# Padding the heads of two activation pools so that activations and split weights share an offset modulo 512 bytes

## The chip, the cores and the metric

The kernel runs on one core of a Trainium2 chip. The metric is the device time of one execution in microseconds. Before the change it is 2132.72 us, the median of 3 runs (2131.33 to 2134.95).

## The reference

One layer of a streaming encoder trunk on x of 256 rows by 2048 features, all in float32, then a last norm.

```python
for l in range(DEPTH):                                   # DEPTH = 1
    h = rms_norm(x, norm_mix_g[l])
    x = x + hybrid_mixer(h, positions, w_in[l], conv_w[l], ..., w_out[l])
    h = rms_norm(x, norm_x_g[l])
    mem_n = rms_norm(mem, norm_mem_g[l])
    x = x + cross_attention(h, mem_n, w_xq[l], w_xkv[l], w_xo[l])
    h = rms_norm(x, norm_ffn_g[l])
    x = x + jnp.square(jax.nn.relu(h @ w_ff1[l])) @ w_ff2[l]
return rms_norm(x, norm_final_g)
```

The mixer projects h once (2048 by 18464 weights) and runs two token mixers side by side, a chunked retention with 8 heads and a gated delta rule with 16 heads; both are gated, merged and projected. The cross-attention has 4 heads over 256 memory rows. The MLP has 8192 hidden features. Nearly all of the work is products of 256 rows with weights of 2048 by some thousand columns.

## The kernel before, in words

Every large product is made in three parts. A float32 operand is split into a high part, rounded by ScalarE to the type that TensorE takes at full rate (L89 for weights, L96 and others for activations), and a low part, the rest, made by VectorE (L90, L97). The product is high by high, high by low and low by high.

Weights come by DMA into `raw` (three buffers of 8192 bytes a partition) and are split in two halves into `whi` and `wlo` (three buffers of 4096 bytes each); the function is `fetch`. Activations lie in quads: `new_quad` makes one tile of 128 partitions by 4 by 512 words, 8192 bytes a partition, which holds four blocks of 128 features; in each block 256 columns of the high part stand beside 256 of the low part.

Two functions multiply.

- `chunk` gives 512 columns of output with rows on the partitions. The activations are the stationary operand (128 columns, 512 bytes), the weights the moving one (512 columns). Each product is three matmuls, L130, L131 and L132. One call is 96 matmuls. It is used for the memory's values, the retention's values, the gates, and the second MLP matrix.
- `blocks` gives 128-column blocks of output with features on the partitions. The weights are the stationary operand (one block of 128 columns, 512 bytes of `whi` or `wlo`), the activations the moving one. A pair of matmuls makes a product: L168 streams 512 columns (high and low part at once) against `whi`, L169 streams 256 columns against `wlo`. One call for two blocks is 32 pairs. It is used for the memory's keys, the mixer's other projections, `w_out`, `w_xq`, `w_xo` and the first MLP matrix.

A matmul of one line is followed at once by that of the next, so the time from a line's first start to its last, divided by the steps between, is the time of one pair or of one triple.

Quads lie in three pools. `hq` (five quads) holds h1, the normed x of the mixer, for the mixer's whole time; then the merged output, the attention's output and the MLP's hidden features. `kv` holds `memq`, four quads of the normed memory, at the start. `q2` holds four quads: h2 (the input of `w_xq`), then h3 (the input of the first MLP matrix). In the very last call of `chunk`, which is called with `hold=quad_b`, the split weights of two of the four fetches go into quads of `q2` too (L84 to L86).

Pools lie one behind the other in each partition, each behind those that are open when it is opened: `const`, `wpipe` (raw, whi, wlo), `hq`, `small`; then `mixc` and `kv` (closed after the memory's keys), in whose place `mix` comes, behind `mixc`; when `mix` and `mixc` are closed, `tail` (the residual, 16384 bytes) comes behind `small`, then `q2`. A pool's size is the sum of its tags, each its largest tile times its buffers.

The order of the instructions on every engine is found before the kernel runs, by a planner that works through the program by priority with estimated durations; a tile with a tag waits for a free buffer of that tag. `blocks` ends with an evacuation of each block in front of other work (`high_priority`): ScalarE writes `bo` (tag `bo`, two buffers), VectorE adds the other half of PSUM, and the caller's function reads `bo`.

In the delta rule's `gdn_stream`, which is called for four groups of two pairs of heads, four small instructions for each pair (L563) take the diagonal of a gram matrix: they write a product that nobody reads into `dj`, and keep its row sums in `ssk`. `dj` is a tile of 512 bytes with a buffer of its own in the pool `mix`.

Of the kernel before, what the change touches and what calls it, by code (L numbers as in the profile page):

```python
# [10 lines left out]
F32 = mybir.dt.float32  # L11
# [6 lines left out]
P = 128  # L18
D = 2048
S = 256  # L20
# [8 lines left out]
C_GQ, C_GK, C_GV = 6144, 8192, 10240  # L29
C_GA, C_GZ, C_TA, C_TB = 12288, 12320, 14368, 16416  # L30
THETA = 10000.0
TWO_PI = 2.0 * math.pi
BIG = 1.0e30


def _short(v, bits):
    m, e = math.frexp(v)
    return math.ldexp(math.floor(m * (1 << bits)), e - bits)


PI_1 = _short(TWO_PI, 12)
PI_2 = _short(TWO_PI - PI_1, 11)
PI_3 = float(np.float32(TWO_PI - PI_1 - PI_2))
MAGIC = 1.5 * 2.0**23
# [3 lines left out]
def trunk(ctx: ExitStack, tc: tile.TileContext, x, mem, positions, norm_mix_g, w_in, conv_w, gdn_a_log, gdn_dt_bias,  # L48
# [4 lines left out]
    act, vec, pool, pe = nc.scalar, nc.vector, nc.gpsimd, nc.tensor  # L53

    cp = ctx.enter_context(tc.tile_pool(name="const", bufs=1))
    wp = ctx.enter_context(tc.tile_pool(name="wpipe", bufs=3))
    hqp = ctx.enter_context(tc.tile_pool(name="hq", bufs=1))
    sm = ctx.enter_context(tc.tile_pool(name="small", bufs=2))
# [8 lines left out]
    def bank():  # L67
        return psp.tile([P, 512], F32, name="b", tag="b", bufs=4)
# [38 lines left out]
    def new_quad(pl, bufs):  # L107
        both = pl.tile([P, 4, 2 * S], F32R, name="q", tag="q", bufs=bufs)
        quad = Quad((both[:, :, 0:S], both[:, :, S:2 * S]))
        quad.both = both  # L110
        return quad
# [137 lines left out]
    kv = kvs.enter_context(tc.tile_pool(name="kv", bufs=2))  # L249
# [18 lines left out]

    kt_d = dram.tile([P, KT, S], F32, name="kt_d", tag="kt_d", bufs=1)
    vv_d = dram.tile([P, NT, D], F32, name="vv_d", tag="vv_d", bufs=1)  # L270
    memq = [new_quad(kv, 4) for _ in range(4)]
    ssqm = cp.tile([P, NT, 4], F32, name="ssqm")

# [87 lines left out]
    def rounded(o, i, scale):  # L361
        vec.tensor_scalar(o, i, scale, MAGIC, op0=ALU.mult, op1=ALU.add)
        vec.tensor_scalar(o, o, -MAGIC, None, op0=ALU.add)

    def less(k, c):
        vec.scalar_tensor_tensor(av, k, -c, av, op0=ALU.mult, op1=ALU.add)

    rounded(hv, av, 1.0 / (4096.0 * TWO_PI))
    less(hv, 4096.0 * PI_1)
    vec.scalar_tensor_tensor(lv, hv, -4096.0 * PI_2, av, op0=ALU.mult, op1=ALU.add)  # L370
    rounded(lv, lv, 1.0 / TWO_PI)
    less(lv, PI_1)
# [131 lines left out]
    mx = mixer.enter_context(tc.tile_pool(name="mix", bufs=2))  # L504
# [14 lines left out]
    def gdn_stream(grp):  # L519
# [5 lines left out]
        for pr in range(2):  # L525
# [16 lines left out]
            for b in range(2):  # L542
                kh = mx.tile([P, 2, S], F32R, name="kh", tag="kh", bufs=2)
                kl = mx.tile([P, 2, S], F32R, name="kl", tag="kl", bufs=2)
                sq = mx.tile([P, S], F32, name="sq", tag="acc", bufs=2)
                act.activation(kh, kq[:, b], AF.Copy)
                vec.tensor_sub(kl, kq[:, b], kh.bitcast(F32))
                act.activation(sq, kq[:, b, 1], AF.Square)
                g0, g1 = bank(), bank()
                g0v = g0.rearrange("p (a n) -> p a n", a=2)  # L550
                g1v = g1[:, 0:256].rearrange("p (a n) -> p a n", a=2)
                if b == 0:
                    ssq = g1[:, 256:260].rearrange("p (b i) -> p b i", b=2)
                for t in range(NT):
                    pe.matmul(ssq[:, b, t:t + 1], sq[:, t * P:(t + 1) * P], ones[:, :1], start=True, stop=True)
                for n, (l, r) in enumerate(((kh, kh), (kh, kl), (kl, kh))):
                    pe.matmul(g0v, l[:, 0, 0:P], r, start=n == 0, stop=n == 2)  # L557
                for n, (l, r) in enumerate(((kh, kh), (kh, kl), (kl, kh))):
                    pe.matmul(g1v, l[:, 0, P:S], r[:, :, P:S], start=n == 0, stop=n == 2)
                grams.append((g0v, g1v))  # L560
                for t, src in enumerate((g0v[:, 0, 0:P], g1v[:, 0, :])):
                    dj = mx.tile([P, P], F32, name="dj", tag="dj", bufs=1)
                    vec.scalar_tensor_tensor(dj, src, 1.0, ident, op0=ALU.mult, op1=ALU.mult,  # L563
                                             accum_out=ssk[:, b, t:t + 1])
            ske = mx.tile([P, 2, NT], F32, name="ske", tag="ske", bufs=2)
# [214 lines left out]
    for j in range(5):  # L780
        if j < 4:
            group = gdn_stream(j)
        if prev is not None:
            if j < 4:
                quad = mx.tile([P, 4, S], F32, name="mg", tag="mg", bufs=3)
                kept.append(quad)
            else:
                quad = quad_a()
            gates(j - 1, prev[0], prev[1], quad, take_back if j == 4 else None)
        if j < 4:  # L790
            yr = mx.tile([P, NT, 512], F32, name="yr", tag="yr", bufs=1)
            yg = mx.tile([P, NT, 512], F32, name="yg", tag="yg", bufs=1)
            retention(j, yr)
            gdn_core(j, *group, yg)
            prev = (yr, yg)
# [5 lines left out]
    tp = ctx.enter_context(tc.tile_pool(name="tail", bufs=2))  # L801
    rt = tp.tile([P, KT, S], F32, name="rt", tag="rt", bufs=1)
    q2p = ctx.enter_context(tc.tile_pool(name="q2", bufs=1))

    def quad_b():
        return new_quad(q2p, 4)
# [181 lines left out]
def _inv_freq():  # L988
    e = np.arange(0, RDK, 2, dtype=np.float32) / np.float32(RDK)
    return (np.float32(1.0) / np.power(np.float32(THETA), e)).astype(np.float32)  # L990

# [17 lines left out]
```

## Time and profile before

| what | value |
| --- | --- |
| median of 3 runs | 2132.72 us (2131.33 to 2134.95) |
| the profiled execution, whole | 2133.46 us |
| its span, first instruction to last | 2131.7 us |
| instructions | 28768 |
| granted TensorE clock, mean | 0.999 |

The profiled execution lies 0.74 us above the median, and 1.8 us of it lie outside the span. Times in rows are microseconds from the start of the span. The busy time of TensorE (PE) counts a matmul until its modelled end, so matmuls overlap in it: the distance of starts, not the duration, is what one costs.

### The profile page before, as it was taken

What the parts mean: (1) busy time and instruction counts of PE and PEld (TensorE: products, weight loads), DVE (VectorE), ACT (ScalarE), POOL (GpSimd) and SP (SyncE); (2) the same over time, 40 slices, a digit from 0 to 9 for tenths busy, and PEclk for the clock granted to TensorE, in tenths of its full rate; (3) what the DMA queues carried; (4) which work ended last, traced back from release to release, by engine and by line L of the source; (5) the groups of instructions that cost most, each with busy time, mean ns of one, the idle gap of its engine ahead of it and who ended that gap; (6) DMA issues with size and microseconds to landing.
All of it is one profiled execution on the core that took longest, in us unless ns stands there. A gap on an engine that the chain in (4) does not pass through costs nothing.

```text
span 2131.7 us, 28768 instructions
## 1 busy us (share of the span) xinstructions
PE 2102.5 (99%) x11172; PEld 1798.5 (84%) x11172; DVE 1411.9 (66%) x2225; ACT 1092.3 (51%) x1700; POOL 30.6 (1%) x39
## 2 busy tenths in 40 slices
PE   8999999899999999999999999999999999999998
PEld 6878888788888888888888888888888888888887
DVE  6756779588678866786567666666556545655655
ACT  7565565364555445645456555554434434434444
POOL 0000000000000000000000000000000000000000
PEclk9999999999999999999999999999999999999999
DMA  8777665455545654565457654566556556556653
GB/s 296 248 235 250 198 194 184 131 172 190 177 148 198 198 187 135 180 203 181 157 178 251 204 180 157 176 188 189 193 189 191 184 193 194 180 197 191 185 197 139
DMA packets 316009, 405.91 MB, mean 190 GB/s; under 512 B 16592, under 2 KB 224480, under 8 KB 315744
## 3 DMA queue, kind: packets, MB, share of 16 engines
q1 hardware_dynamic: 315872, 404.08, 58.6%
q8 instruction: 87, 1.43, 0.3%
q14 instruction: 50, 0.41, 0.1%
HBM read 390.40 MB, written 13.65 MB: 190 GB/s over the span
## 4 chain that ended last, share of the span: by engine, by line
PE 94%; DMA 2%; ACT 1%; DVE 1%; issue 0%; POOL 0%; SPq 0%; ACTq 0%; POOLq 0%; DVEq 0%
PE s L168 32%; PE s L169 16%; PE s L131 13%; PE s L130 13%; PE s L132 13%; PE b L646 2%; DMA dec_d<-dec_w 1%; ACT dec_w L471 1%; PE b L557 1%; PE b L100 0%; ACT whi L89 0%; DVE wlo L90 0%; PE b L102 0%; PE b L101 0%; PE b L215 0%
## 5 line engine op out<-in xcount | busy, mean ns | idle before, releaser
L90 DVE TENSOR_TENSOR wlo<-raw,whi 128x1024 fp32r<-128x1024 f32 x702 | 858.1, 1223 | 523.5 <-ACT whi L89 518.3
L89 ACT ACTIVATE whi<-raw 128x1024 fp32r<-128x1024 f32 x702 | 742.8, 1059 | 724.2 <-PE s L132 370.2
L168 PE MATMUL s<-q,whi 128*128 128x512 f32 x3088 | 1080.1, 397 | 0.3 <-DVE q L898 0.3
L169 PE MATMUL s<-q,wlo 128*128 128x256 f32 x3088 | 845.4, 281 | 6.4 <-DVE wlo L90 6.4
L168 PEld LDWEIGHTS s<-q,whi 128*128 128x128 f32 x3088 | 571.4, 188 | 125.2 <-DVE q L898 0.5
L169 PEld LDWEIGHTS s<-q,wlo 128*128 128x128 f32 x3088 | 580.1, 188 | 21.9 <-DVE wlo L90 10.2
L131 PE MATMUL s<-wlo,q 128*128 128x512 f32 x1264 | 495.3, 392 | 0.2 <-DVE wlo L90 0.2
L132 PE MATMUL s<-whi,q 128*128 128x512 f32 x1264 | 492.0, 390 | 0.0
L130 PE MATMUL s<-whi,q 128*128 128x512 f32 x1264 | 450.1, 391 | 0.0
L131 PEld LDWEIGHTS s<-wlo,q 128*128 128x128 f32 x1264 | 237.9, 188 | 49.8 <-DVE wlo L90 1.2
L130 PEld LDWEIGHTS s<-whi,q 128*128 128x128 f32 x1264 | 237.6, 188 | 50.1 <-ACT q L228 0.4
L132 PEld LDWEIGHTS s<-whi,q 128*128 128x128 f32 x1264 | 237.6, 188 | 48.8
L173 ACT ACTIVATE bo<-s 128x256 f32<-128x256 f32 x193 | 73.1, 379 | 121.6 <-PE s L169 121.6
L174 DVE TENSOR_TENSOR bo<-bo,s 128x256 f32<-128x256 f32 x193 | 80.4, 417 | 54.0 <-ACT bo L173 53.7
L512 DVE SCALAR_TENSOR_TENSOR acc<-bo,cw,acc 128x255 f32<-128x255 f32 (+2 forms) x144 | 67.1, 477 | 4.7 <-ACT acc L509 3.3
L612 DVE TENSOR_TENSOR pr<-lw,tw 32x31 f32<-32x31 f32 (+15 forms) x124 | 40.5, 326 | 9.1 <-DMA lw<-scr_l 6.9
L614 DVE TENSOR_TENSOR tw<-tw,pr 32x31 f32<-32x31 f32 (+15 forms) x124 | 40.7, 328 | 2.4
L747 ACT ACTIVATE gth<-s 128x512 f32<-128x512 f32 x32 | 18.9, 592 | 23.1 <-PE s L132 17.5
L937 DVE SCALAR_TENSOR_TENSOR res<-s,rstd3q,res 128x512 f32<-128x512 f32 (+1 forms) x32 | 22.3, 735 | 12.0 <-PE s L132 12.0
L509 ACT ACTIVATE acc<-bo,cw 128x256 f32<-128x256 f32 x48 | 24.2, 504 | 7.3 <-DVE bo L174 5.1
L926 DVE SCALAR_TENSOR_TENSOR hs<-bo 128x256 f32<-128x256 f32 x64 | 27.0, 422 | 1.1
L929 DVE TENSOR_TENSOR q<-hs,q 128x256 fp32r<-128x256 f32 x64 | 26.8, 418 | 0.9 <-ACT q L928 0.9
(292 smaller groups left out, 1086.7 us busy)
## 6 DMA issues: line engine op xcount, KB each, us to landing
raw<-w_in SPq DMA_DIRECT2D x144, 1024.0 KB
raw<-w_ff SPq DMA_DIRECT2D x128, 1024.0 KB
raw<-w_xkv SPq DMA_DIRECT2D x31, 1024.0 KB
raw<-w_out SPq DMA_DIRECT2D x16, 1024.0 KB
raw<-w_xq SPq DMA_DIRECT2D x16, 1024.0 KB
raw<-w_xo SPq DMA_DIRECT2D x16, 1024.0 KB
dec_d<-dec_w SPq DMA_DIRECT2D x16, 192.0 KB
dec<-dec_d SPq DMA_DIRECT2D x8, 384.0 KB
```

The costliest lines, as they stand in the source:

```text
L89: act.activation(hi, src, AF.Copy)
L90: vec.tensor_sub(lo, src, hi.bitcast(F32))
L130: pe.matmul(o, xh, wh, start=first, stop=False)
L131: pe.matmul(o, xh, wl, start=False, stop=False)
L132: pe.matmul(o, xl, wh, start=False, stop=last)
L168: pe.matmul(ps[b], lh, xhl, start=kk == 0, stop=False)
L169: pe.matmul(ps[b][:, :S], ll, xh, start=False, stop=kk == KT - 1)
L173: act.activation(o, ps[b][:, S:], AF.Copy)
L174: vec.tensor_add(o, o, ps[b][:, :S])
L512: vec.scalar_tensor_tensor(acc[:, d:], ps[:, :S - d], cw[:, j, blk:blk + 1], acc[:, d:], op0=ALU.mult, op1=ALU.add)
L614: vec.tensor_sub(tw[:, j + 1:32, 0:j + 1], tw[:, j + 1:32, 0:j + 1], pv)
L646: pe.matmul(pv[:, i, :], lhs(i), rhs[:, i, :], start=True, stop=True)
```

## The change

Two tiles are made that nothing writes or reads: 8 words (32 bytes a partition) at the head of `kv`, ahead of `memq`, and 80 words (320 bytes) at the head of `q2`, ahead of its quads. The tile `dj` leaves the pool `mix` and becomes the first half of a tile of the tag `bo` in the pool `small`, so that it takes its turn in the two buffers that the evacuations of `blocks` use. What is computed is the same.

```diff
+PAD1, PAD2 = 8, 80
...
     vv_d = dram.tile([P, NT, D], F32, name="vv_d", tag="vv_d", bufs=1)
+    kv.tile([P, PAD1], F32, name="pad1", bufs=1)
     memq = [new_quad(kv, 4) for _ in range(4)]
...
-                    dj = mx.tile([P, P], F32, name="dj", tag="dj", bufs=1)
+                    dj = sm.tile([P, S], F32, name="dj", tag="bo", bufs=2)[:, :P]
                     vec.scalar_tensor_tensor(dj, src, 1.0, ident, op0=ALU.mult, op1=ALU.mult,
                                              accum_out=ssk[:, b, t:t + 1])
...
     q2p = ctx.enter_context(tc.tile_pool(name="q2", bufs=1))
+    q2p.tile([P, PAD2], F32, name="pad2")
```

## Rows read from the trace of the kernel before

**Rows 1.** The page's busy times: us, share of the span, instructions.

```profile
PE 2102.5 (99%) x11172; PEld 1798.5 (84%) x11172; DVE 1411.9 (66%) x2225; ACT 1092.3 (51%) x1700; POOL 30.6 (1%) x39
```

**Rows 2.** The page's chain that ended last, by engine.

```profile
PE 94%; DMA 2%; ACT 1%; DVE 1%; issue 0%; POOL 0%; SPq 0%; ACTq 0%; POOLq 0%; DVEq 0%
```

**Rows 3.** Busy time by stretch; behind the engines: granted clock, DMA share, GB/s.

```profile
114.00:214.00 100.00, 94.41 (x526) 79.33 (x525) 57.27 (x91) 61.48 (x146) 0.00 (x0) 1.00 0.77 245
...
400.00:440.00 40.00, 32.57 (x203) 27.79 (x202) 23.35 (x57) 18.84 (x51) 3.37 (x3) 1.00 0.20 64
...
570.00:625.00 55.00, 55.00 (x365) 50.01 (x364) 37.83 (x69) 28.63 (x55) 2.40 (x3) 1.00 0.46 147
...
795.00:845.00 50.00, 50.00 (x327) 45.22 (x326) 34.49 (x59) 26.74 (x49) 2.34 (x3) 1.00 0.48 153
...
1420.00:2110.00 690.00, 690.00 (x3520) 586.86 (x3519) 400.13 (x481) 309.96 (x398) 0.70 (x1) 1.00 0.59 189
```

**Rows 4.** Line L130 in `chunk` (count, durations, first and last start): values(0), MLP.

```profile
L130 PE MATMUL s<-whi,q x16: 393/396/397, 24.9 to 35.4; 128*128 128x512 f32 x16
L130 PE MATMUL s<-whi,q x33: 389/389/398, 2036.0 to 2057.8; 128*128 128x512 f32 x33
```

**Rows 5.** Busy time, clock and DMA share of three such stretches of `chunk`.

```profile
24.00:36.00 12.00, 12.00 (x55) 9.71 (x54) 9.70 (x22) 7.24 (x13) 0.70 (x1) 1.00 0.89 300
92.00:100.00 8.00, 8.00 (x36) 6.42 (x35) 5.20 (x9) 3.70 (x6) 0.00 (x0) 1.00 0.62 197
...
1682.00:1702.00 20.00, 20.00 (x90) 16.55 (x89) 10.70 (x13) 8.73 (x11) 0.00 (x0) 1.00 0.63 211
```

**Rows 6.** Line L168 in `blocks` with quads of `hq`: `w_in`, `w_in`, `w_out`, `w_xo`.

```profile
L168 PE MATMUL s<-q,whi x152: 389/395/403, 341.2 to 393.9; 128*128 128x512 f32 x152
...
L168 PE MATMUL s<-q,whi x42: 389/398/403, 751.1 to 765.6; 128*128 128x512 f32 x42
...
L168 PE MATMUL s<-q,whi x235: 389/395/478, 1121.5 to 1203.7; 128*128 128x512 f32 x118
...
L168 PE MATMUL s<-q,whi x207: 389/395/497, 1336.6 to 1408.9; 128*128 128x512 f32 x104
```

**Rows 7.** L168 with quads of `kv` (memory's keys) and `q2` (`w_xq`, MLP).

```profile
L168 PE MATMUL s<-q,whi x101: 392/395/402, 177.9 to 213.2; 128*128 128x512 f32 x101
...
L168 PE MATMUL s<-q,whi x36: 388/397/398, 1214.4 to 1226.7; 128*128 128x512 f32 x36
...
L168 PE MATMUL s<-q,whi x256: 388/397/398, 1590.9 to 1680.9; 128*128 128x512 f32 x128
```

**Rows 8.** The last `chunk`: L130 on weights held in `q2`.

```profile
L130 PE MATMUL s<-q x9: 282/394/403, 2112.6 to 2118.2; 128*128 128x512 f32 x8, 128*128 128x256 f32 x1
```

**Rows 9.** Timeline of VectorE and ScalarE around the first four writes of `dj`.

```profile
259.60 0.29 DVE L563 SCALAR_TENSOR_TENSOR dj<-b,ident 128x128 f32<-128x128 f32 x1 [0.32 <-PE b L557]
...
261.27 0.28 DVE L563 SCALAR_TENSOR_TENSOR dj<-b,ident 128x128 f32<-128x128 f32 x1
...
258.44 0.39 ACT L173 ACTIVATE bo<-s 128x256 f32<-128x256 f32 x1 [0.77 <-PE s L169]
...
262.20 0.36 ACT L173 ACTIVATE bo<-s 128x256 f32<-128x256 f32 x1
```

## The prediction

> **What bounds the kernel now.** I read the busy times first: TensorE is busy for 99% of the span, the next engine, VectorE, for 66% [rows 1]. That alone proves little, since overlapping matmuls make a slow TensorE look as busy as a fast one, so I read the chain that ended last: 94% of it is TensorE itself [rows 2]. Then I cut the span into stretches. In the MLP TensorE is busy in all of 690.00 us, while VectorE works 400 and the DMA engines are at 0.59 [rows 3]. Among the stretches shown, TensorE falls short in two: among the memory's keys (5.6 of 100 us) and at the delta rule's first group (7.4 of 40 us) [rows 3]. The granted clock is 1.00, so 2.4 GHz, in every stretch that I use [rows 3, 5]. So the kernel is bound by how closely matmuls follow one another, and a nanosecond saved on each matmul reaches the end nearly whole.
>
> The question is then whether that distance depends on the pool in which an operand lies. Two lines answer it, each with the same program text everywhere. In `chunk`, the sixteen starts of L130 over the memory's quads (pool `kv`) span 10.5 us, 15 triples or 45 matmuls: 233.3 ns each. The 33 starts over hidden features in `hq` span 21.8 us, 96 matmuls: 227.1 ns [rows 4]. Load on the DMA engines does not explain it: they stand at 0.89 in the slow stretch and 0.63 in an MLP stretch of the fast kind. Nor is the slow stretch short of TensorE time: it is busy 12.00 of 12.00 us [rows 5].
>
> In `blocks`, a pair over `hq` takes 52.7/151 = 349.0 ns and 14.5/41 = 353.7 ns (`w_in`), 82.2/234 = 351.3 ns (`w_out`) and 72.3/206 = 351.0 ns (`w_xo`) [rows 6]. Over `kv` it takes 35.3/100 = 353.0 ns, over `q2` 12.3/35 = 351.4 ns (`w_xq`; a start is printed to 0.1 us, so this short row is good to 2.9 ns a pair) and 90.0/255 = 352.9 ns (MLP) [rows 7]. The long rows are good to about 0.5 ns. The order in time is telling: `w_out` (hq), `w_xq` (q2), `w_xo` (hq) and the MLP (q2) alternate, and the two long MLP-like stretches on either side differ by 1.6 to 1.9 ns a pair.
>
> **The offsets.** They follow from the tile shapes. From `whi` to the last quad of `hq` every tile is a multiple of 512 bytes, so `hq` agrees with the weights modulo 512. Behind it `small` takes 2048 + 2048 bytes and six buffers of a word or two, `mixc` 768 + 512 + 1024 + 1024 + 512 + 384 + 128 bytes and one tile of four words. If each of the tiny ones takes 32 bytes, `kv` begins at 480 modulo 512, and `q2` (behind `small` and 16384 bytes) at 192. The pads bring both to 512: 480 + 32 and 192 + 320. So after the change `memq`, h2, h3 and the held weights stand to the weights as `hq` stands now. That is what lets the rows over `hq` price the rest.
>
> **The pads, term by term.** Each is a count times a difference.
> - Memory's values: 4 calls of 96 matmuls, 384 x (233.3 - 227.1) = 2.4 us.
> - First MLP matrix: 4 x 8 calls of 32 pairs, 1024 pairs. The price after is unknown between 349.0 and 353.7, the ends over `hq`. I take 350.4, the mean of the three long rows, since the 353.7 is from 42 pairs alone and two of the long rows run without other products in between, as the MLP does. 1024 x (352.9 - 350.4) = 2.6 us; at the ends 4.0 us and none (353.7 would cost 0.8).
> - `w_xq` and the memory's keys: 256 pairs each. The short row of `w_xq` is too coarse, so I price both as the long `q2` and `kv` rows: 512 x 2.5 = 1.3 us, at the ends 2.0 and -0.4.
> - The last `chunk`: its held part has 24 matmuls of 512 columns, which take 5.6/24 = 233 ns [rows 8], and 48 of half the width. 24 x 6 + 48 x 3 = 0.3 us.
>
> The sum is 2.4 + 2.6 + 1.3 + 0.3 = 6.6 us; with the ends of the pairs 1.5 to 8.7. The pads issue nothing and no transfer changes, so nothing stands against this. Faster products need weights sooner: about 0.8% in the MLP, where the DMA engines stand at 0.59, and 2.6% in the values, where the stretch at 0.89 still leaves a tenth. That cover is enough.
>
> A rule speaks against all of it. The Trainium skill (SBUF — State Buffer, section Who interferes with whom) says that TensorE has two read ports of its own for the moving operand and the weight load, and that it never waits on anyone; by it an operand's offset costs nothing and the time stays at 2132.7 us. The rows over two pools, with one program text, disagree by 6 ns a matmul, which is why the rule is a rival here and not the forecast.
>
> **The move of `dj`.** It happens 32 times, 0.29 us each [rows 9], and costs VectorE the same after. What is new is a wait both ways. `dj` needs a free buffer of `bo`, and an evacuation's ScalarE write of `bo` (L173) must wait until VectorE has left the `dj` in that buffer. In the rows the four `dj` run from 259.60 to 261.55, after the first evacuation (258.44) and before the second (262.20): one buffer holds the first block, the other is free, and the last `dj` is done 0.65 us ahead of the second write. Behind a late L173 on ScalarE stand the weight split and the other half's evacuation, and TensorE waits for those only when its weights or PSUM run out; the PSUM tiles have two buffers each, a call of 32 pairs (11 us) of cover. Below, the cost is nothing; above, 16 places (pairs times heads) of one `dj`, 16 x 0.29 = 4.6 us, if no cover held. I take nothing, since the row shows the gap and the cover is long. But the planner sees a different program, and may order the groups anew; that is the third rival.
>
> **Rivals.**
> 1. The offset is not what differs; the pool's place, or what else runs then, is. For it: the rule above, and that rows over `hq` alone spread over 4.7 ns a pair [rows 6]. Against it: two pools at two different offsets are both slow, and `w_out`, `w_xq`, `w_xo` and MLP alternate. Time: no change, 2132.7 us.
> 2. The alignment works in `chunk` alone, and the pairs fall into the slower of the rhythms seen over `hq`, 353.7 ns [rows 6]. Then 2.4 + 0.3 us are left, less up to 1.2 us for 1536 pairs: some 2130.4 us. For it: aligned pairs are not uniformly fast. Against it: the long aligned rows are all at 351.3 or under.
> 3. Slower: the wait of `dj` makes the planner place the delta rule's serial products closer to the end of their group, with too few pairs between them. The first group already shows this, 7.4 us of TensorE without work, while the second and third show none [rows 3]. One more group exposed would give +7.4 - 6.6 = +0.8 us, no change; it decides from two groups on, +14.9 - 6.6 = +8.3 us, 2141.0 us. Against it: the four instructions are small and followed by nothing urgent.
>
> **How the numbers follow.** The profiled execution takes 2133.46 us, 0.74 above the median; the sum is made against it and moved to the median: 2132.72 - 6.6 = 2126.1 us. Two executions of this kernel can be told apart by about 0.2%, 4.3 us, so faster means under 2128.4 us. Forecast 0.60, rival 1 0.14, rival 2 0.17, rival 3 0.09. The forecast's own range is 2124.0 (every pair at 349.0) to 2128.4. The range for 8 in 10 leaves out rival 3 (0.09) and a tenth on the far side: it reaches up to rival 1 with a little noise, 2133.5, and down to 2121.5, which holds the best pair price and a re-plan that hides a third of the exposed 7.4 us. Rivals 1 and 2 are both within 0.2%: faster 0.60, same 0.31, slower 0.09.
>
> **What would show it.** Values: L130 over `kv` at 227 ns a matmul. MLP: 256 starts of L168 spanning 89.0 to 89.6 us instead of 90.0. Last `chunk`: the held part at 227 ns. `dj`: no idle time of L173 named after L563, and the stretch of the first group still short by about 7 us. The prediction is wrong if the MLP rows stay at 90.0 us, or if TensorE's idle time in the groups grows by more than some microseconds.

## The result and the profile after

The changed kernel takes 2136.58 us (median of 22 runs, 2134.37 to 2145.59) against 2133.33 us for the kernel before (22 runs, 2131.1 to 2140.62, on the same chips). The ratio is 1.0019 with a 95% interval of 1.0011 to 1.0026: slower by 0.2%, where 0.3% faster was forecast. The profiled execution spans 2135.4 us, 3.7 more than before.

Line numbers of the changed kernel are 3 to 5 higher: L133 to L135 are `chunk`'s matmuls, L171 and L172 the pairs of `blocks`, L567 is `dj`, L176 the evacuation's write of `bo`. First its page: the chain that ended last, by engine, to be held against [rows 2].

```profile
PE 91%; DMA 4%; ACT 2%; DVE 1%; SPq 1%; issue 1%; POOL 0%; ACTq 0%; POOLq 0%; DVEq 0%
```

TensorE has lost three points of the chain, two of them to DMA: something now waits for transfers. The rows that answer to [rows 4, 6, 7] say whether the pads did what they were to do. They are, of the changed kernel: the first line of `chunk` in values(0), the pairs over the memory's quads, `w_xq`, one MLP call group, all MLP groups from first to last; then three marks in time, the second group's value projection, the first group's products after its triangular inverse, and the last line of a triple over all four calls of the values.

```profile
L133 PE MATMUL s<-whi,q x16: 388/389/397, 24.9 to 35.6; 128*128 128x512 f32 x16
...
L171 PE MATMUL s<-q,whi x103: 391/395/403, 176.5 to 212.7; 128*128 128x512 f32 x103
...
L171 PE MATMUL s<-q,whi x257: 392/398/477, 1209.9 to 1319.2; 128*128 128x512 f32 x129
...
L171 PE MATMUL s<-q,whi x256: 389/395/403, 1596.6 to 1685.9; 128*128 128x512 f32 x128
...
L171 PE MATMUL s<-q,whi x1025: 389/395/477, 1415.7 to 2039.2; 128*128 128x512 f32 x171
...
L133 PE MATMUL s<-whi,q x32: 389/389/478, 435.0 to 459.6; 128*128 128x512 f32 x32
...
L643 PE MATMUL b<-alt,t x16: 275/275/377, 392.5 to 394.2; 128*128 128x128 f32 x16
...
L135 PE MATMUL s<-whi,q x128: 387/389/628, 11.2 to 114.2; 128*128 128x512 f32 x128
```

Of the kernel before, the rows for `w_xq`, all MLP groups and the three marks, which were not needed so far:

```profile
L168 PE MATMUL s<-q,whi x257: 388/397/483, 1203.7 to 1312.9; 128*128 128x512 f32 x129
...
L168 PE MATMUL s<-q,whi x1025: 388/397/481, 1409.3 to 2035.7; 128*128 128x512 f32 x171
...
L130 PE MATMUL s<-whi,q x33: 389/389/397, 426.9 to 453.0; 128*128 128x512 f32 x33
...
L639 PE MATMUL b<-alt,t x16: 270/275/275, 400.7 to 402.4; 128*128 128x128 f32 x16
...
L132 PE MATMUL s<-whi,q x128: 389/394/628, 11.2 to 114.1; 128*128 128x512 f32 x128
```

The MLP group takes 89.3 us instead of 90.0 [rows 7], 350.2 ns a pair; 350.4 was forecast. In values(0) the median duration fell from 396 to 389 ns, the value that the MLP had in [rows 4], yet sixteen starts still need 10.7 us, 0.2 more than before: the single matmul is quicker and the stretch is not. The pairs of `w_xq` have gained nothing: 109.3 us, and 109.2 before.

With these starts the 3.7 us can be laid out by stretch. Each number is the change of the distance between two such starts, or to the end of the span.

| stretch | before | after | change | forecast |
| --- | --- | --- | --- | --- |
| to the last matmul of the memory's values | 114.1 | 114.2 | +0.1 | -2.4 |
| from there to the last pair of the memory's keys | 99.1 | 98.5 | -0.6 | -0.6 |
| to the second group's value projection (426.9, 435.0) | 213.7 | 222.3 | +8.6 | 0 |
| to the first pair of `w_xq` | 776.8 | 774.9 | -1.9 | 0 |
| `w_xq` | 109.2 | 109.3 | +0.1 | -0.6 |
| to the MLP | 96.4 | 96.5 | +0.1 | 0 |
| MLP to its last pair | 626.4 | 623.5 | -2.9 | -2.6 |
| to the end | 96.0 | 96.2 | +0.2 | -0.3 |

The loss is one stretch, between 213 and 435 us, where no pad is at work. The busy times, to be held against [rows 3], show where in it:

```profile
400.00:440.00 40.00, 32.33 (x182) 27.71 (x183) 23.92 (x59) 19.96 (x54) 3.02 (x3) 0.91 0.20 69
...
570.00:625.00 55.00, 55.00 (x354) 49.56 (x354) 39.98 (x65) 29.44 (x46) 1.39 (x2) 1.00 0.46 146
```

The second group is covered as before. Around the first, TensorE is as idle as it was between 400 and 440 us, but now there is idle time ahead of 400 too, and the granted clock is 0.91. The chain of the changed kernel from 382 to 395 us tells what came late (start, duration, what):

```profile
382.37 2.09 DMA scr_t<-tw
...
387.02 4.53 DMA ct<-scr_t
391.67 0.45 DVE cu L625
392.11 0.32 DVE t L633
392.47 1.84 PE b L643 x14
```

The inverse of the first group's triangular blocks goes out to memory and comes back transposed (`scr_t`, `ct`), and TensorE's next products (L643) need it. They stand at 392.5 us now; they stood at 400.7 us, behind 27 pairs that ran until the transfers had landed. Those pairs, which used to hide the round trip, have been put behind the products.

TensorE then runs for some 30 us at part load, and its clock falls. Busy time and clock of the changed kernel, from 392 us on:

```profile
392.00:412.00 20.00, 13.04 (x95) 1.00 0.12 45
412.00:420.00 8.00, 5.60 (x39) 0.97 0.10 36
420.00:424.00 4.00, 3.22 (x10) 0.50 0.00 0
```

The clock stands at 0.50, so at 1.2 GHz instead of 2.4. The timeline of TensorE brackets the pairs that ran at it:

```profile
420.78 0.80 PE L171 MATMUL s<-q,whi 128*128 128x512 f32 x1 [0.92 <-DVE bo L177]
...
426.58 0.63 PE L171 MATMUL s<-q,whi 128*128 128x512 f32 x2
```

Nine pairs start in between; they take 5.8 us, where nine of 0.35 us are 3.2: 2.6 us more.

The whole loss can be counted between two points by which both kernels have run the same 251 matmuls. Window, length, TensorE's busy time and clock, first before, then after the change:

```profile
391.37:439.44 48.07, 40.80 (x251) 1.00 0.28 88
```

```profile
390.42:446.14 55.72, 44.28 (x251) 0.94 0.26 88
```

That is 7.6 us: TensorE's idle time grows by 4.2 us (7.3 to 11.4), and the same matmuls are busy 3.5 us longer, as a mean clock of 0.94 over 55.72 us would make them (3.3). The other 1.0 of the table's 8.6 us is work that now stands ahead of the mark at 435.0 us; it comes back in the row below. What ended the new idle time (us, times, longest), after the change:

```profile
PE b L643 <- DVE t L633: 1.8, 1, 1.8
...
PE b L563 <- DVE yg L684: 1.4, 1, 1.4
PE s L171 <- DVE bo L177: 0.9, 1, 0.9
PE b L561 <- DVE yg L684: 0.8, 1, 0.8
...
PE b L650 <- ACT am L644: 0.5, 1, 0.5
```

Before, of these lines, only the gram products waited:

```profile
PE b L557 <- DVE yg L680: 1.2, 1, 1.2
```

5.4 less 1.2 are the 4.2 us. 0.9 of them hangs on a `bo`, the rest on products that the new order has put earlier.

The new wait that the prediction weighed is there too. ScalarE's timeline in the changed kernel, two of six such waits:

```profile
260.23 0.39 ACT L176 ACTIVATE bo<-s 128x256 f32<-128x256 f32 x1 [3.31 <-DVE dj L567]
...
420.24 0.39 ACT L176 ACTIVATE bo<-s 128x256 f32<-128x256 f32 x1 [2.09 <-DVE dj L567]
```

Where the evacuation came 1.16 us ahead of the first `dj` [rows 9], it now starts when three of the four are done (the third ends at 260.19). At 260 us nothing follows from it. At 420 us TensorE stands still for 0.9 us until the sum of that `bo` is made (the first of the two rows above): its PSUM tile is the next that it needs.

### The profile page after: what moved, and what is told of

It is laid out like the page before. It is cut to its first block, busy times and chain, and to the rows that moved or that the text cites. A ratio compares the mean times of both kernels' runs of the same rounds, so it can differ in the third digit from the quotient of the medians.

```text
span 2135.4 us, 28778 instructions
## 1 busy us (share of the span) xinstructions
PE 2102.2 (98%) x11172; PEld 1799.1 (84%) x11172; DVE 1410.8 (66%) x2225; ACT 1093.5 (51%) x1700; POOL 29.7 (1%) x39
## 4 chain that ended last, share of the span: by engine, by line
PE 91%; DMA 4%; ACT 2%; DVE 1%; SPq 1%; issue 1%; POOL 0%; ACTq 0%; POOLq 0%; DVEq 0%
PE s L171 32%; PE s L172 16%; PE s L134 13%; PE s L135 12%; PE s L133 12%; PE b L650 2%; DMA dec_d<-dec_w 1%; ACT whi L92 1%; ACT dec_w L475 1%; DVE wlo L93 1%; DMA xc<-x 1%; PE b L561 0%; DMA ct<-scr_t 0%; PE b L103 0%; PE b L104 0%
## 5 line engine op out<-in xcount | busy, mean ns | idle before, releaser
L171 PE MATMUL s<-q,whi 128*128 128x512 f32 x3088 | 1080.2, 397 | 1.2 <-DVE bo L177 0.9
L172 PE MATMUL s<-q,wlo 128*128 128x256 f32 x3088 | 844.4, 281 | 5.3 <-DVE wlo L93 5.1
L171 PEld LDWEIGHTS s<-q,whi 128*128 128x128 f32 x3088 | 572.0, 188 | 126.4 <-DVE bo L177 1.2
L172 PEld LDWEIGHTS s<-q,wlo 128*128 128x128 f32 x3088 | 582.5, 189 | 20.8 <-DVE wlo L93 9.1
L135 PE MATMUL s<-whi,q 128*128 128x512 f32 x1264 | 491.4, 390 | 0.0
L133 PE MATMUL s<-whi,q 128*128 128x512 f32 x1264 | 449.8, 391 | 0.0
L133 PEld LDWEIGHTS s<-whi,q 128*128 128x128 f32 x1264 | 237.4, 188 | 49.6 <-ACT q L231 0.4
L135 PEld LDWEIGHTS s<-whi,q 128*128 128x128 f32 x1264 | 237.7, 188 | 48.5
L176 ACT ACTIVATE bo<-s 128x256 f32<-128x256 f32 x193 | 73.1, 379 | 127.1 <-PE s L172 114.8
L933 ACT ACTIVATE q<-hs 128x256 fp32r<-128x256 f32 x64 | 26.2, 410 | 0.0
```

The costliest lines, as they stand in the source:

```text
L133: pe.matmul(o, xh, wh, start=first, stop=False)
L135: pe.matmul(o, xl, wh, start=False, stop=last)
L171: pe.matmul(ps[b], lh, xhl, start=kk == 0, stop=False)
L172: pe.matmul(ps[b][:, :S], ll, xh, start=False, stop=kk == KT - 1)
L176: act.activation(o, ps[b][:, S:], AF.Copy)
```

## The experiments

Each time stands against that of the kernel before on the same chip. Theory A: the pads pay and the move of `dj` costs, by the order of work and the waits that it brings. Theory B: the pads cost as much as they give. Theory C: offsets change nothing.

**The pads alone.** `dj` stays where it was. Every engine's instructions stand in the same order as before the change.

```diff
-                    dj = sm.tile([P, S], F32, name="dj", tag="bo", bufs=2)[:, :P]
+                    dj = mx.tile([P, P], F32, name="dj", tag="dj", bufs=1)
```

> Both pads, dj left where it was. Theory A (the pads pay, the move of dj costs through the order of work it brings): the first group's delta-rule products stand as before, the first MLP matrix's 256 pairs span 89.3 us instead of 90.0, and the whole is 2129 us (2128 to 2130.5), about 0.2% under before. Theory B (the pads themselves cost as much as they give, by what they do to the start of the kernel or elsewhere): 2133 us or more. Theory C (offsets change nothing): 2133 us with the pairs at 90.0 us.

Measured: 2131.51 us against 2134.22; ratio 0.9989, interval 0.9981 to 0.9998. Its MLP group, and TensorE between 380 and 430 us:

```profile
L169 PE MATMUL s<-q,whi x256: 389/395/404, 1590.5 to 1679.8; 128*128 128x512 f32 x128
```

```profile
380.00:430.00 50.00, 42.73 (x271) 1.00 0.38 117
```

89.3 us, and the first group as before. The MLP row rules C out; against B stands the time, with an interval that ends just under 1. The gain is 2.4 to 2.7 us, not the 4 that A expected from the stretches above, and the time lies above A's range. In this profile the values end at 112.8 us instead of 114.1, but the keys' last pair starts at 213.9 instead of 213.2 [rows 7]: 2.0 us were lost among the keys. TensorE's time there was shorter of work than before, and its clock dipped:

```profile
114.00:214.00 100.00, 93.64 (x517) 79.14 (x516) 56.12 (x84) 60.05 (x144) 0.00 (x0) 0.98 0.79 245
```

The next kernel, without any pad, shows the same clock in this stretch, while the changed kernel, with both, stands at 1.00 and gains 0.6 us among the keys (table above). So the dip is not shown to come from the pads:

```profile
114.00:214.00 100.00, 95.14 (x524) 80.65 (x523) 57.66 (x91) 61.40 (x145) 0.00 (x0) 0.98 0.78 245
```

**`dj` alone.** No pads, `dj` in the turn of `bo`; every engine's order is that of the changed kernel.

> No pad, only dj moved into the turn of bo. Theory A: TensorE loses about 8 us in the first group of the delta rule, 380 to 430 us into the span, with the clock down to 0.5 there for some us, and the whole is 2141 us (2139 to 2143). Theory B (the pads cost, dj is free): 2133 us, and no more loss in the first group than before.

Measured: 2143.42 us against 2134.22; ratio 1.0039, interval 1.0027 to 1.0051, so 8.3 us (9.2 between the medians), a little more than A expected. The MLP group at the old pace, the first group with the new loss:

```profile
L169 PE MATMUL s<-q,whi x256: 388/397/398, 1601.1 to 1691.1; 128*128 128x512 f32 x128
```

```profile
380.00:430.00 50.00, 38.81 (x236) 0.93 0.27 82
```

The same stretch of the kernel before, then of the changed kernel:

```profile
380.00:430.00 50.00, 42.73 (x270) 1.00 0.36 116
```

```profile
380.00:430.00 50.00, 38.56 (x234) 0.93 0.26 82
```

Theory A holds in kind: the halves are +8.3 and -2.4 us. Their sum, 5.9, is more than the 3.3 us between the medians of the whole change. The three intervals are wide enough to allow both, and no run settles whether the halves simply add.

**Three buffers for `bo`.** Both pads, `dj` shared as in the change.

```diff
-    o = sm.tile([P, S], F32, name="bo", tag="bo", bufs=2)
+    o = sm.tile([P, S], F32, name="bo", tag="bo", bufs=3)
...
-                    dj = sm.tile([P, S], F32, name="dj", tag="bo", bufs=2)[:, :P]
+                    dj = sm.tile([P, S], F32, name="dj", tag="bo", bufs=3)[:, :P]
```

> Both pads, dj in the tag bo as in the change, but three buffers for that tag. On the chip a third buffer takes away any wait of an evacuation for a dj or of a dj for an evacuation; the order of the instructions stays nearly the one of the changed kernel (TensorE's differs in 8 of 10585 rows). If the loss comes from the order: about as the changed kernel, 2136.6 us (2134 to 2139). If it comes from waits for the two buffers while the kernel runs: 2129 us.

Measured: 2144.93 us against 2134.22; ratio 1.0047, interval 1.0031 to 1.0064. It is slower than either theory said, and its premise was false: four `dj` fill three buffers as well, and ScalarE still waits for them (us, times):

```profile
  ACT bo L174: 8.4, 5
```

So it doesn't tell the order from the waits. It shows that one more buffer doesn't heal the sharing.

**Two buffers of its own.** Both pads, `dj` in `mix` under its own tag.

```diff
-                    dj = mx.tile([P, P], F32, name="dj", tag="dj", bufs=1)
+                    dj = mx.tile([P, P], F32, name="dj", tag="dj", bufs=2)
```

> Both pads, dj in the pool mix under its own tag as before, but with two buffers. If the loss comes from dj having two buffers instead of one (four small writes that need no longer follow one another): as the changed kernel, 2136 us. If it comes from dj taking its turn among the evacuations' buffers, which puts it ahead of the next evacuation: as the pads alone, 2129 us.

Measured: 2131.24 us against 2134.22; ratio 0.9986, interval 0.9975 to 0.9996, as the pads alone. The cost comes from the shared turn and not from the number of buffers. (The change also moved `dj` to the pool `small`; no run gave it a tag of its own there.)

**The opposite placing.** `hq` 32 bytes off the weights, `memq` and `q2` aligned; order as before.

```diff
+    hqp.tile([P, 8], F32, name="pad0")
...
+    q2p.tile([P, 72], F32, name="pad2")
```

> The opposite placing: h1 and all other quads of hq 32 bytes off the weights modulo 512, the memory's quads and q2 aligned (pads of 8 words in hq and 72 in q2, none in kv); the order of all instructions is that of the kernel before. If the offset modulo 512 sets the pace: the MLP's second-matrix calls of chunk go from 227 to 233 ns a matmul, 36 calls of 96 at 6.4 ns, 22 us more than with the pads alone, and pairs over hq go to 351 to 353 ns; the whole is 2151 to 2157 us. If what matters is the pool and not the offset: hq keeps 227 ns, and the whole is 2129 to 2133 us.

Measured: 2147.5 us in a single run, under the 2151 to 2157 expected; its span is 2145.8. `chunk` over hidden features (first line, one MLP group of four calls), and the pairs of `w_out`:

```profile
L132 PE MATMUL s<-whi,q x128: 392/395/396, 1510.4 to 1599.3; 128*128 128x512 f32 x128
...
L170 PE MATMUL s<-q,whi x256: 389/390/476, 1122.4 to 1211.9; 128*128 128x512 f32 x128
```

88.9 us for 381 matmuls, 233.3 ns each: the offset sets the pace of `chunk`, in the pool that had been the fast one. But the pairs did not get slower, though that was expected; they take 89.5 us where `w_out` took 90.3 before (1113.4 to 1203.7). That is a surprise worth a run (below).

**Half of 512.** `hq` 256 bytes off, the rest aligned; order as before.

```diff
+    hqp.tile([P, 64], F32, name="pad0")
...
+    kv.tile([P, 72], F32, name="pad1", bufs=1)
...
+    q2p.tile([P, 16], F32, name="pad2")
```

> As the run before it with half of 512 bytes: hq stands 256 bytes off the weights, the memory's quads and q2 are aligned; same order of instructions as the kernel before. If only an equal offset modulo 512 is fast: 233 ns in chunk over hq and 2151 us or more. If the pace repeats every 256 bytes, or the pool is what matters: 227 ns and 2129 to 2133 us.

Measured: 2129.24 us in a single run. The same MLP group:

```profile
L132 PE MATMUL s<-whi,q x128: 389/389/398, 1501.7 to 1588.1; 128*128 128x512 f32 x128
```

86.4 us, 226.8 ns a matmul. 256 bytes are as good as none: 512 in the change's wording is a multiple of what counts.

**No loads of x, without and with the pads.** The four loads of x are left out and the memory's rows stand in for x, so another output is computed.

```diff
-    xcs = [load_rows(c, x, 0) for c in range(4)]
+    xcs = mem_rows
```

> No pads, and the four loads of x (512 KB each) at the start are left out: the rows of the memory stand in for x, so the output is another. It is the ground for the next run. The values' calls of chunk stay at 233 ns a matmul; the time is 2130 to 2134 us.

> The same without the loads of x, but with both pads; its order of instructions is that of the run before. If the values' and keys' gain was lost because the loads of x and of the weights pace that stretch: without them the second pair of calls ends about 2 to 3 us earlier than in the run before, and the two kernels differ by 5 to 6 us, instead of 2.5. If something else takes it back (the evacuations, the planned order): still 2 to 3 us between the two.

Measured: 2135.08 us (10 runs; 2130 to 2134 was expected) and 2130.5 us (10 runs) on one chip, spans 2132.5 and 2127.3. The last line of a triple over all four calls of the values, first without, then with pads; the third row is from the pads alone, with the loads of x:

```profile
L133 PE MATMUL s<-whi,q x128: 389/396/478, 11.1 to 115.4; 128*128 128x512 f32 x128
```

```profile
L133 PE MATMUL s<-whi,q x128: 388/389/628, 11.0 to 114.1; 128*128 128x512 f32 x128
```

```profile
L133 PE MATMUL s<-whi,q x128: 387/389/629, 11.4 to 112.8; 128*128 128x512 f32 x128
```

Without the loads of x the values gain 1.2 us (104.3 to 103.1). With them the pads alone gain as much: 102.9 before becomes 101.4. So the loads of x are not what keeps the values from gaining the forecast 2.4. The two kernels differ by 4.6 us (spans 5.2), short of the 5 to 6 expected. That is more than the pads alone gave, but the difference doesn't lie in the values: neither of these two profiles has a dip of the clock among the keys. It is one profile of each.

**Pairs with a lead of 32 bytes.** From the opposite placing: `q2`, which only pairs stream from but for the last call, stands 32 bytes ahead; `hq` and `memq` aligned, `dj` as before the change.

```diff
+    kv.tile([P, 8], F32, name="pad1", bufs=1)
...
+    q2p.tile([P, 88], F32, name="pad2")
```

> Pads of 8 words in kv and 88 in q2, dj left where it was: h2 and h3 stand 32 bytes ahead of the weights modulo 512, hq and the memory's quads are aligned. If a lead of 32 bytes of the moving operand is what made pairs over hq take 347.6 ns when hq stood there: the 256 pairs of an MLP call group span 88.6 us (90.0 before, 89.3 aligned), and the whole is 3 us under the pads alone, 2128 us, 5 to 6 us under before. If it was hq itself: 89.3 us or more, and 2131 us.

Measured: 2126.21 us against 2134.86; ratio 0.9967, interval 0.9956 to 0.9979: 7 us, more than the 5 to 6 expected. It beats both kernels. `w_xq` gains too: 107.8 us (1202.8 to 1310.6) instead of 109.2. The MLP group takes 88.6 us, 347.5 ns a pair:

```profile
L169 PE MATMUL s<-q,whi x256: 390/390/399, 1587.2 to 1675.8; 128*128 128x512 f32 x128
```

**64 and 128 bytes** for `memq` and `q2`, `hq` aligned (pads of 24 and 96 words, and of 40 and 112).

> hq aligned, the memory's quads and q2 64 bytes off the weights modulo 512. If the pace repeats every 64 bytes: 227 ns a matmul in the values and 89.3 us for 256 MLP pairs. If it repeats every 128 or 256 bytes, like the 192 bytes of before: 90.0 us for the pairs, and 233 ns in the values.

> hq aligned, the memory's quads and q2 128 bytes off. If the pace repeats every 128 bytes: 227 ns in the values and 89.3 us for 256 MLP pairs, and a rest of 32, 64 or 96 bytes is what counts. If only every 256 bytes: 90.0 us or another value.

Measured: 2131.46 and 2131.27 us in a single run each. Their MLP groups, one row of each kernel:

```profile
L169 PE MATMUL s<-q,whi x256: 388/394/399, 1590.3 to 1679.8; 128*128 128x512 f32 x128
```

```profile
L169 PE MATMUL s<-q,whi x256: 387/396/398, 1590.0 to 1679.5; 128*128 128x512 f32 x128
```

89.5 us each, 351 ns a pair: neither the 90.0 of 192 bytes nor the 89.3 of none. The first line of `chunk` in the last call of the values, at 64 bytes, at 128, and aligned (the pads alone):

```profile
L131 PE MATMUL s<-whi,q x32: 391/394/398, 91.5 to 113.6; 128*128 128x512 f32 x32
```

```profile
L131 PE MATMUL s<-whi,q x32: 388/393/404, 92.6 to 114.7; 128*128 128x512 f32 x32
```

```profile
L131 PE MATMUL s<-whi,q x32: 388/389/397, 90.8 to 112.4; 128*128 128x512 f32 x32
```

22.1 us at both, 21.6 aligned. The pace doesn't repeat within 128 bytes.

## Why the prediction was wrong

**The move of `dj`: this step failed.** It was taken as nothing because the row showed the last `dj` 0.65 us ahead of the second evacuation [rows 9], and its upper end was 4.6 us, by waits alone. Measured: 8.3 us. Two things were overlooked. First, sharing a tag means taking buffers in turn, so the four `dj` take theirs ahead of the next evacuation, and ScalarE waits up to 3.31 us for them. Second, the end of the range was priced by waits, though the text itself said that the planner sees another program; a new order can cost more than the instruction that causes it. It moved the first group's products by 8 us ahead of the pairs that had hidden the `ct` round trip, and the clock fell behind the idle time. In the changed kernel that is 3.3 us of idle time and 3.5 us of slower matmuls, where the wait for a `bo` cost TensorE 0.9 us. This division rests on what the trace names; no run separates the order from the waits.

**Rival 3 had the new order, and neither its direction nor its place.** It let the products come later in their group and priced exposed groups beyond the first. They came earlier. None was exposed newly; the first, already short of 7.4 us [rows 3], got worse, and the half clock, which no term held, nearly doubled the price. That its +8.3 us is also what `dj` alone cost is luck: it stands for two groups less the pads.

**The pads: right in kind, too large in sum.** 6.6 us were forecast, 2.4 to 2.7 measured, 2.0 of the rest lost in the profile with the dip among the keys. The MLP's term was right (2.6, measured 2.9), and in the changed kernel the keys' (0.6 and 0.6). Three were not.
- Values (2.4; 1.5 in the pads alone, none in the changed kernel): the matmul got quicker as forecast, and where triples follow one another their step fell from 700 to 680 ns. The prediction let every matmul of the stretch gain that, since a tenth of the DMA engines' time was left as cover. In the changed kernel TensorE waited there for split weights, as it had not before:

```profile
PE s L134 <- DVE wlo L93: 1.1, 2, 0.6
```

  What takes the rest of the gain in the pads alone stays open; it is not the loads of x.
- `w_xq` (0.6, none): its aligned pairs still take 109.3 us. Before, 189 of 228 steps there, from the start of one pair to the next, take 353 or 354 ns; after, most take about 350, but 66 take 360 or 361. In the short row over `hq` that showed 353.7 ns [rows 6], 13 of 39 steps take 361. So that row was no accident, as the prediction took it; in the MLP, too, 42 of 235 aligned steps take 360 or 361.
- The last call (0.3, none): its matmuls of 512 columns went from 233 to 227 ns, as forecast. The 48 of half the width, priced at 3 ns each without a row, went the other way, from 114 to 120 ns, which is 0.3 us.

**Rival 2 is near in time by luck.** Its 2130.4 us is close to the 2131.5 of the pads alone, but the MLP's pairs went to 350.2 ns and not to 353.7; only `w_xq` behaved as it said.

**Rival 1, that offsets don't matter, is out.** With one order of instructions, a matmul of `chunk` took 226.8 ns at 256 bytes and 233.3 ns at 32. The Trainium skill (SBUF — State Buffer, section Who interferes with whom) has TensorE never wait on anyone; that is said of engines that work at the same time, and the prediction's reading, that an offset then costs nothing, is what the runs refute.

## What to carry to other kernels

A tile that only moves to another tag is not free: its turn among that tag's buffers is a dependency, and it can reorder a planned program; compare the order of instructions before pricing such an edit by its duration. A gain in TensorE's pace is not worth its full size in a stretch where split weights come just in time, even if TensorE is busy all the time there. Where matmuls run back to back, the distance between stationary and moving operand modulo 256 bytes is worth one run each at a few values. The best one differed here between `chunk` (none) and `blocks` (activations 32 bytes ahead); whether that comes from which operand is the activation or from the shapes, no run separates.

## What the runs showed of the hardware

The pace of matmuls depends on where the stationary and the moving operand start. With activations as the stationary operand, a matmul of 512 columns takes 226.8 ns when both agree modulo 256 bytes and 233.3 ns at 32 bytes, whether the activations stand ahead (the opposite placing) or behind (the memory's quads before the change); at 64 and 128 bytes the last call of the values is as slow, 22.1 us against 21.6. With activations as the moving one, a pair of 512 and 256 columns takes 350 ns when they agree, 347.5 ns with a lead of 32 bytes, 351 ns at 64 and at 128, 353 ns at 192 and at 32 bytes behind [rows 7]. The offsets are worked out from the tile shapes, each tiny tile taken as 32 bytes; no profile prints an address. What in the chip makes this so, no run here shows.

The granted clock fell to 0.50 in the middle of the kernel, at 420 us, behind a stretch in which TensorE was busy for 13.04 of 20 and then 5.60 of 8 us. In the kernel before it stayed at 1.00 in the same windows:

```profile
392.00:412.00 20.00, 17.07 (x111) 1.00 0.50 165
412.00:420.00 8.00, 4.91 (x36) 1.00 0.00 0
```
